# Sparse attention with queries scaled ahead of the split, compressed scores as one 32-column product, and a third pair of FFN blocks by seven products

## The chip, the cores and the metric

The kernel runs on one core of one Trainium2 chip. The metric is the device time of one execution in microseconds. The core's engines are called by their short names in the profile: PE (TensorE: matmuls and transposes into PSUM), PEld (PE's weight loads), DVE (VectorE), ACT (ScalarE), POOL (GpSimd) and SP (SyncE, which issues most DMAs here). Each engine works through its own queue in order and waits for the others by semaphores.

## The reference, cut to what matters

256 tokens, width 1024, two layers. Layer 0 is FFN, stick-breaking attention, FFN; then one shared set of keys and values is computed, with a compression of overlapping blocks of 32 tokens into 15 "compressed" tokens; layer 1 is FFN, sparse attention (16 heads in 4 groups), FFN. All in float32.

```python
h = h + 0.5 * _swiglu(_rmsnorm(h, ffn1_norm[layer]), ffn1_w_in[layer], ffn1_w_out[layer])
...
kvs = _nsa_shared_kv(h, kv_norm, nsa_w_kv, nsa_k_norm, ...)
...
q = _apply_rope(_rmsnorm(q, q_norm), cos, sin)                      # per head, 64 wide
s_c = einsum(q, k_c) * scale                                        # 15 compressed tokens
p_c = softmax(where(valid_c, s_c, NEG)) * any(valid_c)
o_c = einsum(p_c, v_c)
o_s = _nsa_selected(q, sel_idx, k_s, v_s)                           # all 4 blocks of 64 are selected here
o_w = _nsa_window(q, k_w, v_w)
o = gates[0] * o_c + gates[1] * o_s + gates[2] * o_w
```

## The kernel before, in words

**Precision.** Every float32 operand x is split into two float32r parts, hi = round(x) (a copy on ACT) and lo = x - hi (a subtraction on DVE). A product is then three matmuls: hi·hi, hi·lo, lo·hi (`mm3`, L290 to L292). PE does nearly nothing else, and DVE and ACT spend most of their time on splitting weights.

**Weights.** The class `Weights` holds one list of all weight units (128 x 1024, 512 KB) in the order in which they are used. SP loads a unit into a raw buffer, ACT writes its hi (`wh`, L222) and DVE its lo (`wl`, L226), six units ahead at most. `take` hands out the next unit, `done` frees it, `pump` starts the split of a further one. For pairs by seven, some units are sums of weights, which DVE forms beside the splits (L221, L228, L234). A list of jobs, one a unit, also issues DMAs that prepare such sums for the last FFN in DRAM (`far_sums`: moves on SP, L335, and accumulating DMAs on POOL, L338).

**FFN.** The hidden width of 2816 is 11 blocks of 256. A plain block (`proj_block`) is four pieces of twelve matmuls with 512 columns, two for each half of the tokens, and uses four weight units. A "pair by seven" (`pair`) computes two blocks with seven products of twelve matmuls instead of eight, in the manner of Strassen: it uses sums of quarters of the activations (`sums_of_h`) and of the weights, 14 units. A "chunk" is one unit of the second matrix of the FFN (12 matmuls, 22 chunks in all), and chunks are put between the products so that PE has work while DVE prepares weights. The table `FAST` writes this out by hand: a number is a plain block; a tuple is a pair, whose digits are its products, `c` a chunk, `m` a transpose of the gated result (`gtrans`), and `s` a step of the list `side`.

**The changed FFN (f11)**, the first of layer 1: seven plain blocks, then pairs (7, 8) and (9, 10). Beside its plain blocks run the 15 steps of `side` from `kv_phase`: norm and rope of the keys (`k_norm`, `k_scale`, `k_rope`), and the compression: transposes (`c_trans`), the addition of positions on POOL (`c_blocks`, L1224), the split (`c_split`, L1229 and L1230), the hidden product on PE in four steps of two weight units (`c_hidden`, L1246), and what follows it. Step 0 comes after the second piece of the first block; two steps are done per block, after its second and its fourth piece.

**Sparse attention.** The queries are projected in three blocks of heads (`Q_BLOCKS`: head pairs 0-1, 2-4, 5-7). `q_evac` takes them out of PSUM and squares them; `q_turn` applies rope (POOL, L1375 to L1379), splits them (L1380, L1381) and computes the inverse norm `rq` (L1385 to L1392). hi and lo of a head lie side by side, so that one transposed tile `qs` (`q_trans`, L1402 and L1404) holds both along the contraction, and the keys `kD` hold their hi (and their lo) twice along it: two matmuls, against `kh` and `kl`, make a full product. `scores(n)` does the score matmuls of head n for both halves of the tokens (L1417): a mask product, 272 columns (256 keys, 16 compressed) for the first half, 512 keys and 16 compressed columns for the second. Then come the maxima (L1434, L1435), their product with `rq` (L1437), four Exps (L1440, L1445) with the maxima as bias and `rq` as scale, a copy of the compressed scores (L1442), and the normalisation on POOL (L1453). `cmp_soft` is the softmax of the compressed scores of four heads, `ptrans` transposes the probabilities (L1492 to L1495), `values` multiplies by the values. The loop over n puts scores four heads ahead of values; from head 12 on chunks of the output projection come between.

**Order.** A scheduler orders each engine's instructions by their place in the program and by the time at which it expects their inputs; `keep_in_program_order` pins an instruction behind the one traced before it on its engine.

## Time and profile before

| | us |
|---|---|
| three runs | 995.5, 997.32, 995.35; median 995.5 |
| the profiled execution, device time | 994.79 |
| its span, first to last instruction | 993.0 |
| PE busy in the span | 983.4 |
| DVE busy | 873.7 |
| ACT busy | 698.2 |
| POOL busy | 114.9 |

The granted clock of PE is 1.00 throughout. How to read the rows that follow: a group is line, engine, operation, output<-inputs, shape and count, then busy us and the mean ns of one, then the engine's idle time just before and what ended most of it. A row in the order of time is start and length in us, then the same, with the idle time ahead in square brackets. A row of stages is the stretch, its length, and for each engine its busy us with the count of instructions. Durations of neighbouring instructions on one engine overlap, so what one costs is the distance from its start to the next one's.

### The profile page before, as it was taken

To read this page: it belongs to the slowest core of one execution; us is meant where nothing else is said; L and a number is where in the kernel's file an instruction comes from. 1 tells how busy PE (TensorE), PEld (TensorE's weight loads), DVE (VectorE), ACT (ScalarE), POOL (GpSimd) and SP (SyncE) were. 2 spreads that over 40 slices of the span, in tenths; PEclk is the share of its full clock that TensorE was granted. 3 is DMA by queue.
4 is the path that set the end of the run, shared out by engine and by line. 5 is a ranking of instruction groups with operands and counts; after the bars stand their busy time and mean duration, and the time that the engine had idled before them with its cause. 6 is when DMAs were issued, how large, how long until landed. Compare 5 with 4: busy or idle time off the path is not lost.

```text
span 993.0 us, 14093 instructions
## 1 busy us (share of the span) xinstructions
PE 983.4 (99%) x4961; PEld 817.1 (82%) x4961; DVE 873.7 (88%) x1149; ACT 698.2 (70%) x1099; POOL 114.9 (12%) x184
## 2 busy tenths in 40 slices
PE   9999999999999999999999999999999999999998
PEld 6787888898988788878888887888897888788887
DVE  7899999878879999999778698898668879999996
ACT  6776767577868767777565775666669958767763
POOL 0000000010000000000217101000056500000000
PEclk9999999999999999999999999999999999999999
DMA  9988774599846978775996789667330186977761
GB/s 332 355 244 254 222 211 144 176 303 292 247 151 225 332 230 250 235 208 171 273 318 206 252 278 245 235 207 219 114 121 1 45 311 228 310 231 216 250 170 43
DMA packets 65479, 219.89 MB, mean 221 GB/s; under 512 B 7168, under 2 KB 9216, under 8 KB 65408
## 3 DMA queue, kind: packets, MB, share of 16 engines
q1 hardware_dynamic: 58336, 197.86, 58.3%
q0 software_dynamic: 6784, 20.97, 12.1%
q8 instruction: 39, 0.64, 0.3%
q14 instruction: 32, 0.26, 0.1%
q10 hardware_dynamic: 288, 0.16, 0.1%
HBM read 212.67 MB, written 13.63 MB: 228 GB/s over the span
## 4 chain that ended last, share of the span: by engine, by line
PE 69%; issue 13%; DVE 8%; DMA 4%; ACT 3%; POOL 2%; SPq 0%; ACTq 0%; DVEq 0%; POOLq 0%
PE o L291 6%; PE o L292 6%; PE o L290 6%; PE c L290 5%; PE c L292 5%; PE c L291 5%; DVE wl L226 4%; PE a L290 3%; PE a L292 2%; PE a L291 2%; PE cu L290 2%; PE cu L292 2%; PE cu L291 2%; DMA keep<-in_f1i 2%; PE qk L948 2%
## 5 line engine op out<-in xcount | busy, mean ns | idle before, releaser
L226 DVE TENSOR_TENSOR wl<-wraw,wh 128x1024 fp32r<-128x1024 f32 (+2 forms) x316 | 377.1, 1210 | 37.4 <-ACT wh L222 35.7
L222 ACT ACTIVATE wh<-wraw 128x1024 fp32r<-128x1024 f32 (+2 forms) x316 | 322.6, 1044 | 71.1 <-PE o L292 23.8
L222 ACT ACTIVATE wh<-keep 128x1024 fp32r<-128x1024 f32 x112 | 116.6, 1056 | 68.5 <-DVE keep L234 48.8
L226 DVE TENSOR_TENSOR wl<-keep,wh 128x1024 fp32r<-128x1024 f32 x112 | 132.7, 1216 | 6.2 <-ACT wh L222 5.9
L234 DVE TENSOR_TENSOR keep<-keep,wraw 128x1024 f32<-128x1024 f32 x80 | 97.2, 1215 | 1.6 <-DMA wraw<-in_f1i 1.6
L291 PE MATMUL o<-wl,gTh0f 128*128 128x512 f32 x192 | 75.0, 391 | 0.3 <-DVE wl L226 0.3
L290 PE MATMUL o<-wh,gTh0f 128*128 128x512 f32 x192 | 74.8, 397 | 0.0
L292 PE MATMUL o<-wh,gTl0f 128*128 128x512 f32 x192 | 74.6, 391 | 0.0
L290 PE MATMUL o<-wh,gTh1f 128*128 128x512 f32 (+1 forms) x160 | 62.5, 399 | 0.0
L291 PE MATMUL o<-wl,gTh1f 128*128 128x512 f32 (+1 forms) x160 | 62.1, 388 | 0.0
L292 PE MATMUL o<-wh,gTl1f 128*128 128x512 f32 (+1 forms) x160 | 61.3, 388 | 0.0
L290 PE MATMUL a<-wh,hT_f 128*128 128x512 f32 x144 | 57.5, 399 | 0.0
L290 PE MATMUL c<-wh,hT_f 128*128 128x512 f32 x144 | 56.6, 393 | 0.0
L292 PE MATMUL a<-wh,hT_f 128*128 128x512 f32 x144 | 56.3, 391 | 0.0
L291 PE MATMUL a<-wl,hT_f 128*128 128x512 f32 x144 | 56.3, 391 | 0.0
L291 PE MATMUL c<-wl,hT_f 128*128 128x512 f32 x144 | 56.2, 390 | 0.0
L292 PE MATMUL c<-wh,hT_f 128*128 128x512 f32 x144 | 56.2, 390 | 0.0
L290 PE MATMUL cu<-wh,sums 128*128 128x512 f32 x112 | 44.6, 398 | 1.0 <-ACT cp L754 1.0
L290 PE MATMUL c<-wh,sums 128*128 128x512 f32 x112 | 44.3, 396 | 0.1
L292 PE MATMUL cu<-wh,sums 128*128 128x512 f32 x112 | 43.8, 391 | 0.0
L292 PE MATMUL c<-wh,sums 128*128 128x512 f32 x112 | 43.7, 390 | 0.0
L291 PE MATMUL c<-wl,sums 128*128 128x512 f32 x112 | 43.6, 389 | 0.0
(346 smaller groups left out, 2365.0 us busy)
## 6 DMA issues: line engine op xcount, KB each, us to landing
wraw<-in_f1i SPq DMA_DIRECT2D x76, 512.0 KB, 4.8
wraw<-in_f2i SPq DMA_DIRECT2D x68, 512.0 KB, 5.0
wraw<-in_f1o SPq DMA_DIRECT2D x44, 512.0 KB, 4.7
wraw<-in_f2o SPq DMA_DIRECT2D x44, 512.0 KB, 4.8
wraw<-in_sbqk SPq DMA_DIRECT2D x16, 512.0 KB, 4.6
wraw<-sf SPq DMA_DIRECT2D x16, 512.0 KB, 4.5
keep<-in_f2i SPq DMA_DIRECT2D x16, 512.0 KB, 4.5
keep<-in_f2i POOLq DMA_DIRECT2D x16, 512.0 KB, 8.8
```

The source lines that it names most:

```text
L222: i = nc.scalar.activation(hi[:, 0:n], raw[:, 0:n], AF.Copy)
L226: e.tensor_tensor(lo[:, 0:n], raw[:, 0:n], hi[:, 0:n].bitcast(F32), op=OP.subtract)
L234: nc.vector.tensor_tensor(t, y, raw, op=OP.add)
L290: nc.tensor.matmul(o, xh, wh, start=start, stop=False, skip_group_check=True)
L291: nc.tensor.matmul(o, xh, wl, start=False, stop=False, skip_group_check=True)
L292: nc.tensor.matmul(o, xl, wh, start=False, stop=stop, skip_group_check=True)
L948: nc.tensor.matmul(oi, wh[:, c], xh, start=k == 0 and q == 0, stop=False, skip_group_check=True)
```

## The change

Three things are changed together.

1. Blocks 5 and 6 of f11 become a pair by seven; there are five plain blocks and three pairs. The chunks among the pairs are 5, 5 and 6 instead of 7 and 8. The 15 side steps are done three to a plain block (`SIDES`), after its second, third and fourth piece, and the compression's eight weight units move in the list of units (`CMP_AT`).
2. The queries are multiplied by their inverse norm ahead of the split. `q_turn` becomes four steps (rope, norm, scale, split); for query blocks 0 and 1 they are done at once, with rope and scale on DVE, for block 2 one by one in the loop over heads, with rope and scale on POOL. The norm's last steps move from POOL to DVE. The scale drops out of the Exps, and the products of the maxima and of the compressed scores with `rq` are gone.
3. The compressed keys' lo is stored a second time next to the second copy of the hi, so that the second half's two products with 16 columns are one with 32 columns. Its two halves are added later, for four heads at a time (`cmp_max`, split off from `cmp_soft`). `cmp_trans` moves behind `values`.

The letters `p` and `P`, by which a pattern could give a unit's split to POOL, are used in no pattern.

```diff
-CMP_J = 4
+CMP_AT = (12, 12, 14, 16)
+SIDES = (1, 2, 3)
...
-        "f11": (0,1,2,3,4,5,6,(7,"cs1ccm5cc3c67c24"),(9,"cm1cmc5cc3cc67c24")),
+        "f11": (0,1,2,3,4,(5,"1ccm5c3c67c24"),(7,"mc1cm5c3c67c24"),(9,"mc1cmc5c3c67c24")),
...
-    units.extend(f1i1[:4 * CMP_J])
-    cw = len(units)
-    for i in range(4):
-        units.extend(a["cmp"][j] for j in range(2 * i, 2 * i + 2))
-        units.extend(f1i1[4 * CMP_J + 2 * i:4 * CMP_J + 2 * i + 2])
-    units.extend(f1i1[4 * CMP_J + 8:])
+    for i, n in enumerate(CMP_AT + (len(f1i1),)):
+        units.extend(f1i1[CMP_AT[i - 1] if i else 0:n])
+        if i < 4:
+            units.extend(a["cmp"][j] for j in range(2 * i, 2 * i + 2))
...
-                        if i % 2 == 1 and side:
+                        if i in SIDES and side:
...
+            nc.vector.tensor_tensor(kD[0][:, :, 528:544], pv, hi.bitcast(F32), op=OP.subtract)
...
+                e = nc.vector if h0 < 10 else nc.gpsimd
+                return [lambda: q_rope(qv, n, e), lambda: q_norm(sq, n, h0), lambda: q_scale(qv, n, h0, e), lambda: q_split(hi, qv)]
...
+            def q_scale(qv, n, h0, e):
+                e.tensor_tensor(qv, qv, rq[:, :, h0:h0 + n].unsqueeze(3).to_broadcast([P, 2, n, DH]), op=OP.mult)
...
-                nc.gpsimd.tensor_tensor(z, y, y, op=OP.mult)
-                nc.gpsimd.tensor_tensor(z, z, v, op=OP.mult)
-                nc.gpsimd.tensor_scalar(z, z, -0.5, 1.5, op0=OP.mult, op1=OP.add)
-                nc.gpsimd.tensor_tensor(r, y, z, op=OP.mult)
+                nc.vector.tensor_tensor(z, y, y, op=OP.mult)
+                nc.vector.scalar_tensor_tensor(z, z, -0.5, v, op0=OP.mult, op1=OP.mult)
+                nc.vector.scalar_tensor_tensor(r, z, 1.5, y, op0=OP.add, op1=OP.mult)
...
-                mm(sa[:, 272:288], q1, kh[:, 256:272])
                 mm(sv, q1, both(kh), True)
-                mm(sa[:, 272:288], q1, kl[:, 256:272])
                 mm(sv, q1, both(kl))
+                mm(sa[:, 272:304].rearrange("p (t c) -> p t c", t=2), q1,
+                   kh.rearrange("p (t c) -> p t c", t=2)[:, :, 256:272])
...
-                m = nm[:, 0, :].rearrange("p (t b) -> p t b", t=2)
-                nc.vector.tensor_tensor(m, m, r.unsqueeze(2).to_broadcast([P, 2, 2]), op=OP.mult)
...
-                                         scale=r[:, 0:1], accum_out=nm[:, 1, b:b + 1])
+                                         accum_out=nm[:, 1, b:b + 1])
...
+            def cmp_max(sc):
+                nc.vector.tensor_tensor(cs[sc][:, 1], cs[sc][:, 1], cs[sc][:, 2], op=OP.add)
...
-                nc.gpsimd.tensor_tensor(cs[sc], cs[sc], rq[:, :, 4 * sc:4 * sc + 4].unsqueeze(3).to_broadcast([P, 2, 4, 16]),
-                                        op=OP.mult)
...
                 if n == 1:
-                    turn()
-                if n == 3:
+                    rope()
+                if n == 4:
                     q_trans(2, (5,))
...
                 if n + 4 < 16:
                     scores(n + 4)
+                if n == 1:
+                    norm()
+                if n == 2:
+                    scale()
+                if n == 3:
+                    split()
...
                 values(n - 1)
+                if n % 4 == 3:
+                    cmp_trans(sc)
```

More of the change, by code (lines that the diff above doesn't have):

```diff
@@ L82, in __init__ @@
         self.key, self.load, self.join, self.last = key, load, join, last
-        self.more = ()
+        self.more, self.slow = (), False
 class Unit:
@@ L90, in __init__ @@
         self.ap, self.key, self.of, self.hold, self.held = ap, key, of, hold, held
-        self.more = ()
+        self.more, self.slow = (), False
 class Weights:
@@ L224, in pump @@
             self.tc.keep_in_program_order(i)
-        e = nc.gpsimd if u in self.on_pool else nc.vector
+        e = nc.gpsimd if not isinstance(x, bass.AP) and x.slow else nc.vector
         e.tensor_tensor(lo[:, 0:n], raw[:, 0:n], hi[:, 0:n].bitcast(F32), op=OP.subtract)
@@ L403, in fast @@
                     v += b(n.pop(0), 1)
+                elif ch in "pP":
+                    for d in range(-1 - (ch == "P"), 0):
+                        if isinstance(v[d], bass.AP):
+                            v[d] = Unit(v[d])
+                        v[d].slow = True
                 elif ch in "tx":
@@ L480, in build @@
     msb = cp.tile([P, P], BF, name="msb")
-    mns = cp.tile([P, 320], BF, name="mns")[:, 0:288]
+    mns = cp.tile([P, 320], BF, name="mns")[:, 0:304]
     def consts():
@@ L492, in consts @@
         nc.vector.tensor_copy(mns[:, 256:288], msk[:, M_C:M_C + 32])
+        nc.gpsimd.memset(mns[:, 288:304], 0.0)
     ssq = {}
@@ L1344, in nsa @@
                 nc.gpsimd.memset(x[64:128].bitcast(F32), 0.0)
-            qw, Pm, PT, cs, Ox = {}, {}, {}, {}, {}
+            qw, Pm, PT, cs, cm, Ox = {}, {}, {}, {}, {}, {}
             heads = [(2 * sc + i, hh) for sc in range(4) for hh in range(2) for i in range(2)]
@@ L1409, in scores @@
                 if n % 4 == 0:
-                    cs[sc] = sp.tile([P, 2, 4, 16], F32, tag="cs", bufs=2, name="cs")
+                    cs[sc] = sp.tile([P, 3, 4, 16], F32, tag="cs", bufs=2, name="cs")
                 g = 2 * (p // 4) + hh
@@ L1420, in scores @@
                 sv = sb.rearrange("p (t c) -> p t c", t=2)
-                mm(sa[:, 0:288], identb, mns, True)
+                mm(sa[:, 0:304], identb, mns, True)
                 mm(sa[:, 0:272], q0, kh[:, 0:272])
                 mm(sa[:, 0:272], q0, kl[:, 0:272])
-                mm(sa[:, 272:288], q1, kh[:, 256:272])
                 mm(sv, q1, both(kh), True)
-                mm(sa[:, 272:288], q1, kl[:, 256:272])
                 mm(sv, q1, both(kl))
+                mm(sa[:, 272:304].rearrange("p (t c) -> p t c", t=2), q1,
+                   kh.rearrange("p (t c) -> p t c", t=2)[:, :, 256:272])
                 mm(sb[:, 256:512], identb, mns[:, 0:256])
@@ L1446, in scores @@
                                          vb[:, b, :, :], AF.Exp, bias=nm[:, 0, 2 + b:3 + b],
-                                         scale=r[:, 1:2], accum_out=nm[:, 1, 2 + b:3 + b])
+                                         accum_out=nm[:, 1, 2 + b:3 + b])
                 f = nm[:, 2, :].rearrange("p (t b) -> p t b", t=2)
@@ L1453, in scores, with cmp_soft @@
                     nc.gpsimd.tensor_tensor(x, x, nm[:, 2, j:j + 2].unsqueeze(2).to_broadcast([P, 2, w]), op=OP.mult)
-            def cmp_soft(sc):
-                v = cs[sc].rearrange("p t n i -> p (t n) i")
-                mx = sp.tile([P, 2, 8], F32, tag="cm", bufs=2, name="cm")
+            def cmp_max(sc):
+                nc.vector.tensor_tensor(cs[sc][:, 1], cs[sc][:, 1], cs[sc][:, 2], op=OP.add)
+                v = cs[sc][:, 0:2].rearrange("p t n i -> p (t n) i")
+                mx = cm[sc] = sp.tile([P, 2, 8], F32, tag="cm", bufs=2, name="cm")
                 nc.vector.tensor_reduce(mx[:, 0, :], v, axis=AX.X, op=OP.max)
                 nc.gpsimd.tensor_tensor(v, v, mx[:, 0, :].unsqueeze(2).to_broadcast([P, 8, 16]), op=OP.subtract)
-                nc.gpsimd.tensor_tensor(cs[sc], cs[sc], rq[:, :, 4 * sc:4 * sc + 4].unsqueeze(3).to_broadcast([P, 2, 4, 16]),
-                                        op=OP.mult)
+            def cmp_soft(sc):
+                v = cs[sc][:, 0:2].rearrange("p t n i -> p (t n) i")
+                mx = cm[sc]
                 nc.scalar.activation(v, v, AF.Exp)
@@ L1536, in nsa @@
                 turn = q_evac(b, o)
-                if b < 2 or not True:
-                    turn()
+                while b < 2 and turn:
+                    turn.pop(0)()
+            rope, norm, scale, split = turn
             oo = None
@@ L1571, in nsa @@
                 if n == 1 or n % 4 == 0:
+                    cmp_max(sc)
                     cmp_soft(sc)
-                if n % 4 == 3:
-                    cmp_trans(sc)
                 if n + 1 < 16:
```

17 lines of the change are left out of this document (8 added, 9 removed).

## The prediction, made before the changed kernel was run

> **What bounds the kernel now.** I read the page first, for the engines' shares, then busy time by stage, then groups of instructions by shape, last the order of time around the places that the change touches.
>
> ```profile
> PE 983.4 (99%) x4961; PEld 817.1 (82%) x4961; DVE 873.7 (88%) x1149; ACT 698.2 (70%) x1099; POOL 114.9 (12%) x184
> ```
>
> TensorE (PE) is busy for 983.4 of 993.0 us. Since matmuls are pipelined, that alone does not say that a removed matmul shortens the run; the stages do. The next rows are busy time by stage: the second FFN of layer 0 (310 to 440), the plain blocks of the FFN that changes (515.9 to 610), its two pairs (610 to 690), the query projection (710 to 745.5) and the sparse attention's heads (745.5 to 789).
>
> ```profile
> core 0: us, PE busy (x) PEld busy (x) DVE busy (x) ACT busy (x) POOL busy (x), PEclk, DMA share, GB/s
> 310.00:440.00 130.00, 129.18 (x583) 105.30 (x582) 128.00 (x141) 97.41 (x124) 7.59 (x9) 1.00 0.82 258
> ...
> 515.90:568.00 52.10, 52.10 (x252) 43.50 (x251) 41.35 (x53) 33.14 (x45) 23.77 (x28) 1.00 0.76 226
> 568.00:610.00 42.00, 41.93 (x225) 34.50 (x224) 34.05 (x46) 27.45 (x37) 2.27 (x6) 1.00 0.88 283
> 610.00:690.00 80.00, 80.00 (x358) 65.61 (x358) 73.38 (x75) 53.92 (x65) 0.90 (x1) 1.00 0.69 217
> ...
> 710.00:745.50 35.50, 35.26 (x231) 32.48 (x230) 26.95 (x57) 26.49 (x65) 15.45 (x32) 1.00 0.41 130
> 745.50:789.00 43.50, 41.33 (x275) 34.57 (x274) 34.84 (x92) 42.28 (x158) 27.92 (x56) 1.00 0.03 9
> ```
>
> From 515.9 to 690 PE idles 0.07 us: there the run gets shorter by what PE is spared, if VectorE (DVE) keeps up. From 745.5 to 789 ScalarE (ACT) is busy for 42.28 of 43.50 us and PE idles 2.17: ACT sets that stage, and PE's savings alone are worth little in it.
>
> **The third pair by seven.** Two plain blocks are 96 matmuls of 512 columns; a pair is seven products of twelve, 84. Neighbours in the order of time start 0.23 us apart:
>
> ```profile
> 604.08 0.39 PE L291 MATMUL a<-wl,hT_f 128*128 128x512 f32 x1
> 604.31 0.39 PE L292 MATMUL a<-wh,hT_f 128*128 128x512 f32 x1
> ```
>
> 12 x 0.23 = 2.8 us less on PE. The price is on DVE (rows of the two pairs, 610 to 690):
>
> ```profile
> L226 DVE TENSOR_TENSOR wl<-wraw,wh 128x1024 fp32r<-128x1024 f32 x29 | 34.6, 1217 | 1.9 <-ACT wh L222 1.7
> ...
> L234 DVE TENSOR_TENSOR keep<-keep,wraw 128x1024 f32<-128x1024 f32 x8 | 9.7, 1215 | 1.6 <-DMA wraw<-in_f1i 1.6
> L221 DVE TENSOR_TENSOR wraw<-wraw,wraw 128x1024 f32<-128x1024 f32 x4 | 4.9, 1219 | 0.1
> ...
> L656 DVE SCALAR_TENSOR_TENSOR g<-x,sil 128x256 f32<-128x256 f32 x4 | 1.7, 418 | 0.0
> L759 DVE TENSOR_TENSOR x<-cu,cp 128x512 f32<-128x512 f32 x2 | 1.4, 684 | 0.0
> ```
>
> A pair takes 14 weight units where two blocks take 8: six more splits at 1.22, eight sums of weights (L234 and L221's kind) at 1.22 and two sums of results at 0.68, together 18.5 us of DVE, and six splits and four copies on ACT, which is busy for 53.9 of 80 there. Cover: DVE idles 10.8 + 8.0 + 6.6 = 25.4 us between 515.9 and 690, so it would be busy for about 96% of it. The 310 row shows this kernel with DVE at 128.0 of 130 us and PE idle for 0.82. Lower bound 0. Upper bound: the pairs by themselves, with nothing ready ahead. The third pair and the one chunk more that is put among the pairs bring 15 splits and 8 sums at 1.22, four passes at 0.68 and four gates at 0.42, 32.5 us, against PE's eight products of twelve and two transposes, 23; 73.4 + 32.5 is 3 us over PE's 80 + 23. I take 0.8, the 310 row's, as the nearest. DMA: two transfers of 512 KB more on SP's queue, since the pair reads one quarter of its weights twice; the share of the DMA engines is 0.69 there, so 0.
>
> **One 32-column product.** Per head, two 16-column products become one of 32 columns:
>
> ```profile
> 727.63 0.51 PE L1417 MATMUL S<-kDh,qs 128*128 128x16 f32 x2
> 727.97 0.51 PE L1417 MATMUL S<-kDl,qs 128*128 128x16 f32 x2
> 728.32 0.28 PE L1417 MATMUL S<-mns,identb 128*128 128x256 bf16 x1
> ...
> L1417 PE MATMUL S<-mns,identb 128*128 128x288 bf16 x16 | 4.7, 294 | 0.3 <-ACT cs L1442 0.3
> L1417 PE MATMUL S<-mns,identb 128*128 128x256 bf16 x16 | 4.5, 281 | 0.0
> ```
>
> A pair of 16 and 512 columns takes 0.34 us from start to start, 0.11 more than 512 alone; 16 x 0.11 = 1.8 us of PE. The mask's 16 more columns cost at most 13 ns a head (288 against 256), 0.1 in all, set against it. The evacuated scores grow by 16 columns and get one small addition per four heads.
>
> **Norm ahead of the split.** With the queries scaled beforehand, the 64 Exps lose their per-partition scale, 16 small DVE products go, and four POOL products:
>
> ```profile
> L1440 ACT ACTIVATE P<-S,nm,rq 128x128 f32<-128x128 f32 x32 | 15.0, 486 | 0.8 <-DVE nm L1437 0.8
> L1445 ACT ACTIVATE P<-S,nm,rq 128x256 f32<-128x256 f32 x32 | 18.4, 602 | 0.0
> L1463 ACT ACTIVATE cs<-cs 128x128 f32<-128x128 f32 x4 | 1.3, 325 | 0.7 <-POOL cs L1461 0.7
> L1359 ACT ACTIVATE qsq<-qp,rstd 128x384 f32<-128x384 f32 x4 | 2.4, 591 | 2.7 <-DVE qw L1356 2.7
> L1494 ACT ACTIVATE PT<-pt 128x384 fp32r<-128x384 f32 x16 | 8.0, 506 | 0.9 <-PE pt L1492 0.9
> ...
> L1437 DVE TENSOR_TENSOR nm<-nm,rq 128x4 f32<-128x4 f32 x16 | 3.3, 207 | 0.2
> L1461 POOL TENSOR_TENSOR cs<-cs,rq 128x128 f32<-128x128 f32 x4 | 1.6, 405 | 0.3
> ```
>
> No row shows this Exp with one operand less. An Exp of the same shape with neither bias nor scale takes 325 ns (L1463) against 486 (L1440): 161 for two, 80 for one. A Square with a scale takes 591, a Copy of that shape without one 506: 85. Lower bound 0 (the functions and the sources differ), upper 85. I take 80: 64 x 0.08 = 5.1 us of ACT, of which 48 Exps of twelve heads, 3.8 us, lie between 745.5 and 789. The Trainium skill (ScalarE: Activation LUTs, What ACT_TABLE_LOAD costs) gives about 93 ns for each such operand; by that the 64 are worth 6.0 us, the stage below would reach PE's bound of 3.5, and the sum would be -5.4.
>
> What is late next there is PE: it needs 41.33 - 12 x 0.11 = 40.0 us, so the stage can shrink by 3.5 at most. DVE (34.8) and POOL (27.9) have room. I take 3.0, since PE and ACT alternate in dependence. The heads ahead of 745.5 give 4 x 0.11 = 0.4, on a PE that idles 0.24 us. Together -3.4; bounds -0.4 and, with the other 16 Exps' 1.3 us and the whole 3.5, -5.2.
>
> Against it stands a longer way of the first queries. Rope moves from POOL to DVE for query blocks 0 and 1, and the norm comes ahead of the split:
>
> ```profile
> 719.38 1.06 POOL L1375 TENSOR_TENSOR qr<-qw,cst 128x128 f32<-128x128 f32 x1 [5.08 <-DVE qw L1356]
> ...
> 721.06 0.46 POOL L1379 TENSOR_TENSOR qw<-qr 128x128 f32<-128x128 f32 x1
> ...
> 720.43 0.67 DVE L1385 TENSOR_REDUCE qn<-qsq 128x8 f32<-128x512 f32 x1
> ...
> 722.22 0.69 DVE L1381 TENSOR_TENSOR qw<-qw 128x512 f32<-128x512 f32 x1 [0.46 <-ACT qw L1380]
> ...
> 724.28 1.03 PE L1402 MATMUL qTp<-cst,qw 128*128 128x128 f32 x8
> ...
> 727.07 0.34 PE L292 MATMUL qp<-wh,hT_m 128*128 128x384 f32 x1
> ```
>
> Rope's four steps take 2.1 us on POOL; on DVE four at 0.2 (L1437's) are 0.8. Added are a reduction of 0.67, six small steps of 0.2 on DVE and ACT, and a scaling like L1381's 0.69: 2.6. The transposes that follow (724.28) come 1.3 us later; the projection's last piece, up to 727.07, can go ahead of them, so it costs 0, and 1.3 if PE's order keeps the transposes first. Block 2's rope stays on POOL, its scaling goes there too (six times L1461's size: 2.4 us), and its steps spread over the first three heads; the scores that need it are those of head 8, four heads later: 0.
>
> **The compression beside five blocks.** Fifteen side steps now lie beside five plain blocks, three a block, and the first product of the compression (L1246) comes after 11 pieces of plain block instead of 16:
>
> ```profile
> 525.31 3.90 POOL L1224 TENSOR_TENSOR kvb<-kvb,vec 128x120 f32<-128x120 f32 x4
> ...
> 539.62 0.98 POOL L338 DMA_DIRECT2D sf<-in_f2i  x1
> 547.65 0.91 POOL L338 DMA_DIRECT2D sf<-in_f2i  x1 [7.05 <-DMA wraw<-in_cmp]
> 549.12 1.68 POOL L1224 TENSOR_TENSOR kvb<-kvb,vec 128x120 f32<-128x120 f32 x4 [0.56 <-DVE hT_xb L1230]
> ...
> 558.61 1.05 ACT L1229 ACTIVATE hT_xb<-kvb 128x1024 fp32r<-128x1024 f32 x1
> ...
> 559.87 1.22 DVE L1230 TENSOR_TENSOR hT_xb<-kvb,hT_xb 128x1024 fp32r<-128x1024 f32 x1
> ...
> 562.74 0.28 PE L1246 MATMUL hid<-wh,hT_xb 128*128 128x256 f32 x1
> ```
>
> Five pieces of 12 x 0.23 and a transpose step of 0.4 are 14.2 us, so the product falls due at 548.5 instead of 562.7. It needs the eight additions for the second half (L1224) and their split (L1229, L1230: 2.3 us). The additions of 549.12 were released by DVE's split of the first half, not by the DMA issue that ends 0.56 us ahead of them. That split moves up by three pieces, 8.3 us, to about 540.7; additions (2 x 1.68) and split then end at 546.4, in time. Bounds: 0, and the 10 us that the slower rival works out. I take 0.5, near the lower end, by that row.
>
> **Sum.** -2.8 + 0.8 - 3.4 + 0.5 = -4.9. The profiled execution took 994.8, so 989.9; the runs' median of 995.5 is 0.7 above it, so 990.6, put at 990.5.
>
> **Rivals.** *POOL's queue delays the compression (slower).* The accumulating DMA of 547.65 sits 7.05 us in POOL's queue behind the one of 539.62. If the additions stand behind it, as now, they begin at 548.6 however early their input is, and end with their split 5.7 us later if they go as at 549.12, or 10.1 later if as at 525.31 (3.90 for four): 5.8 to 10.2 us after they are due. With no other work for PE the middle, 8, makes -5.4 + 8.0 = +2.6: 998.1. It decides for slower from a stall of 7.4 us on. The Trainium skill (GPSIMD Engine Reference, Key points) says that GpSimd shares its SBUF interfaces with VectorE and contends with its two-input instructions; 3.90 against 1.68 us for the same four would fit it, and by that rule the longer end holds, 10.2, and 1000.3. Against the rival: 549.12 names DVE, not the queue, and PE may take the next piece first. *DVE becomes the bound of the three pairs.* It is at 73.4 of 80 already; at its upper 3 us the pair earns nothing: 992.8. The 310 row speaks against it. *The heads do not shrink.* If the Exps' time does not fall, or PE's waits there are of order and not of ACT, only 0.4 remains of 3.4: 993.6.
>
> **Chances.** The forecast 0.57 (988 to 992.5); the heads 0.15 (half faster, half within 0.2%); DVE 0.13 (0.08 faster, 0.05 within); POOL's queue 0.15 (0.09 slower, 0.06 within). The 0.2%, 2 us, is about what a measurement of this kernel tells from no change. Faster 0.72, same 0.19, slower 0.09. The range goes from 987.5 (all gains at their ends and no new stall, -8.0) to 997 (the lower part of the queue rival).
>
> **What would show it.** Exps near 406 and 522 ns; ACT no longer over 95% busy through the heads, PE above it; the heads' stage near 40.5 us; 12 matmuls of 512 columns and 16 of 16 columns fewer; DVE about 96% busy in the changed FFN with PE idle under 1 us; no idle of PE ahead of L1246's product. A PE wait there, or on weight splits in the first of the three pairs, or Exps of the same length, would make me wrong.

## The result, and the profile after

The changed kernel takes 1003.19 us (median; 1002.68 to 1003.47), the kernel before 995.51 beside it: ratio 1.007, 95% interval 1.0056 to 1.0085. The forecast was 990.5, so the change is slower where I had given that 0.09. Measured once more on another chip it was 1003.52, ratio 1.0075 (1.0057 to 1.0092).

I cut both profiled executions at three products of TensorE: the first of the changed FFN, the first of the query projection, the first of the last FFN. These rows are from the order of time, first of before, then of after (start, duration, engine, line, operation).

```profile
515.87 0.39 PE L290 MATMUL a<-wh,hT_f 128*128 128x512 f32 x1
...
710.26 0.39 PE L290 MATMUL qp<-wh,hT_m 128*128 128x304 f32 x1
...
816.43 0.48 PE L290 MATMUL a<-wh,hT_f 128*128 128x512 f32 x1
```

```profile
516.89 0.39 PE L290 MATMUL a<-wh,hT_f 128*128 128x512 f32 x1
...
718.43 0.39 PE L290 MATMUL qp<-wh,hT_m 128*128 128x304 f32 x1
...
824.67 0.48 PE L290 MATMUL a<-wh,hT_f 128*128 128x512 f32 x1
```

| stage, us | before | after | difference | forecast |
|---|---|---|---|---|
| up to the changed FFN | 515.9 | 516.9 | +1.0 | 0 |
| changed FFN, compression beside it | 194.4 | 201.5 | +7.1 | -1.5 |
| sparse attention | 106.2 | 106.2 | 0.1 | -3.4 |
| last FFN to the end | 176.6 | 177.0 | +0.4 | 0 |

The first row is no effect of the change: nothing is different up to there, and over the profiled executions of this study the changed FFN (or its counterpart) starts between 514.3 and 517.5, but for the one kernel that changes an earlier FFN. The second execution of the changed kernel has 516.0 there, and again 201.5 for the FFN.

The page's line of shares after:

```profile
PE 980.2 (98%) x4933; PEld 811.8 (81%) x4933; DVE 893.3 (89%) x1173; ACT 700.2 (70%) x1109; POOL 110.9 (11%) x162
```

The 28 matmuls are gone (4961 to 4933), as forecast. The time went into waits. These are TensorE's waits in the changed FFN after (who waits, for whom: us in all, times, longest; the longer ones), first beside the plain blocks, then in the three pairs:

```profile
PE xtp L1212 <- DVE kva L1209: 1.8, 1, 1.8
PE gTp L669 <- DVE kDl L1196: 0.9, 1, 0.9
PE gTp L669 <- DVE g L661: 0.7, 1, 0.7
```

```profile
PE c L291 <- DVE wl L226: 1.5, 1, 1.5
PE cu L290 <- ACT cp L757: 1.5, 1, 1.5
```

Before, the stage had PE idle for 0.07 us up to 690. Two different places, then: transposes of the compression and of the plain blocks that wait for VectorE, and products of the pairs that wait for weights or for a copy.

### The profile page after: what moved, and what is told of

Same layout as the page of the kernel before. It is cut to its first block, busy times and chain, and to the rows that moved or that the text cites. A ratio compares the mean times of both kernels' runs of the same rounds, so it can differ in the third digit from the quotient of the medians.

```text
span 1001.7 us, 14034 instructions
## 1 busy us (share of the span) xinstructions
PE 980.2 (98%) x4933; PEld 811.8 (81%) x4933; DVE 893.3 (89%) x1173; ACT 700.2 (70%) x1109; POOL 110.9 (11%) x162
## 4 chain that ended last, share of the span: by engine, by line
PE 63%; issue 15%; DVE 11%; DMA 5%; ACT 2%; POOL 2%; SPq 0%; DVEq 0%; POOLq 0%; ACTq 0%
PE o L291 6%; PE o L292 6%; PE o L290 6%; PE c L290 5%; PE c L292 5%; PE c L291 5%; DVE wl L226 5%; PE cu L290 2%; PE cu L292 2%; PE cu L291 2%; DMA wraw<-in_f1i 2%; PE qk L951 2%; PE qk L952 1%; PE qk L953 1%; PE gTp L669 1%
## 5 line engine op out<-in xcount | busy, mean ns | idle before, releaser
L222 ACT ACTIVATE wh<-keep 128x1024 fp32r<-128x1024 f32 x120 | 125.5, 1056 | 70.5 <-DVE keep L234 49.5
L226 DVE TENSOR_TENSOR wl<-keep,wh 128x1024 fp32r<-128x1024 f32 x120 | 142.4, 1217 | 7.2 <-ACT wh L222 6.8
L234 DVE TENSOR_TENSOR keep<-keep,wraw 128x1024 f32<-128x1024 f32 x84 | 102.1, 1216 | 1.9 <-DMA wraw<-in_f1i 1.9
L292 PE MATMUL o<-wh,gTl0f 128*128 128x512 f32 x192 | 74.5, 391 | 0.0
L291 PE MATMUL c<-wl,hT_f 128*128 128x512 f32 x156 | 61.1, 392 | 1.5 <-DVE wl L226 1.5
L290 PE MATMUL c<-wh,hT_f 128*128 128x512 f32 x156 | 61.3, 393 | 0.0
L292 PE MATMUL c<-wh,hT_f 128*128 128x512 f32 x156 | 60.8, 390 | 0.0
L290 PE MATMUL a<-wh,hT_f 128*128 128x512 f32 x112 | 45.1, 402 | 0.0
L291 PE MATMUL a<-wl,hT_f 128*128 128x512 f32 x112 | 43.9, 392 | 0.0
L292 PE MATMUL a<-wh,hT_f 128*128 128x512 f32 x112 | 43.8, 391 | 0.0
```

Of the source, the lines that this page charges most:

```text
L222: i = nc.scalar.activation(hi[:, 0:n], raw[:, 0:n], AF.Copy)
L226: e.tensor_tensor(lo[:, 0:n], raw[:, 0:n], hi[:, 0:n].bitcast(F32), op=OP.subtract)
L234: nc.vector.tensor_tensor(t, y, raw, op=OP.add)
L290: nc.tensor.matmul(o, xh, wh, start=start, stop=False, skip_group_check=True)
L291: nc.tensor.matmul(o, xh, wl, start=False, stop=False, skip_group_check=True)
L292: nc.tensor.matmul(o, xl, wh, start=False, stop=stop, skip_group_check=True)
```

## The experiments

Theory: the FFN part of the change carries the loss, half of it by the denser side steps, half by the third pair; the sparse attention gains what was forecast and gives it back in its last heads. All times are medians; the ratio is to the kernel before on the same chip.

| run | us | ratio, 95% | changed FFN | sparse attention |
|---|---|---|---|---|
| ffn_only | 1000.75 | 1.0035 to 1.0065 | 200.8 | 106.1 |
| sides_only | 998.98 | 1.0022 to 1.0049 | 198.3 | 106.1 |
| ffn_late | 999.43 | 1.0024 to 1.0050 | 197.1 | 105.8 |
| nsa_only | 994.97 | 0.9986 to 1.0006 | 194.4 | 107.5 |
| norm_only | 993.57 | 0.9973 to 0.9992 | 194.3 | 104.2 |
| nsa_cmp | 992.27 | 0.9951 to 0.9976 | 194.5 | 103.7 |
| nsa_cmp_n | 994.27 | 0.9979 to 1.0000 | 194.4 | 106.0 |
| nsa_add | 993.60 | 0.9970 to 0.9991 | 194.4 | 105.7 |
| combo | 995.20 | 0.9989 to 1.0006 | 198.1 | 103.7 |
| after_again | 1003.52 | 1.0057 to 1.0092 | 201.5 | 107.5 |
| ffn_skip7 | 1000.91 | 1.0039 to 1.0064 | 200.3 | 106.1 |
| skip_mid | 999.77 | 1.0028 to 1.0055 | 195.5 | 106.1 |
| skip_all | 997.56 | 1.0013 to 1.0032 | 195.4 | 106.2 |
| pair_mid | 1003.25 | 1.0064 to 1.0088 | 199.3 | 106.1 |
| pair_cp2 | 1002.18 | 1.0054 to 1.0082 | 200.1 | 105.9 |
| combo_mid | 995.61 | 0.9991 to 1.0013 | 199.8 | 103.8 |
| ffn_pool | 1018.89 | 1.0216 to 1.0256 | 218.4 | 106.0 |
| f20_narrow | 1001.12 | 1.0041 to 1.0066 | 194.3 | 106.1 |

The stage columns are the profiled execution's, cut as above.

### Which part carries the loss

**The FFN part alone (ffn_only).** Before, with this edit:

```
-CMP_J = 4
+CMP_AT = (12, 12, 14, 16)
+SIDES = (1, 2, 3)
...
-        "f11": (0,1,2,3,4,5,6,(7,"cs1ccm5cc3c67c24"),(9,"cm1cmc5cc3cc67c24")),
+        "f11": (0,1,2,3,4,(5,"1ccm5c3c67c24"),(7,"mc1cm5c3c67c24"),(9,"mc1cmc5c3c67c24")),
...
-                        if i % 2 == 1 and side:
+                        if i in SIDES and side:
```

> The kernel before with only the FFN part of the change (third pair by seven, three side steps of the compression beside each of five plain blocks). Theory A, the FFN part carries the loss: its stage was 7.2 us longer in the changed kernel (201.5 against 194.4 from its first product to the first of the query projection), so about 1002.7, +7. Rival B, the sparse attention's part carries it, by way of what it does to weights and buffers around it: then about 993 to 995.

**The sparse attention's part alone (nsa_only).** After, with the lines above put back.

> The changed kernel with its FFN part undone: norm ahead of the split and the 32-column product alone. Theory A: the stage took 106.2 us before and after, so 995.5 within 1.0, although the Exps are shorter by 90 ns each. Rival B: 999 or more. My prediction's own step would give 992.1 (-3.4).

**The side steps alone (sides_only).** As ffn_only, with before's f11 line: five blocks with three side steps each, two without, two pairs.

> The kernel before with two pairs as it had them, and only the compression packed three side steps beside each of the first five plain blocks (two plain blocks and the pairs then follow without side steps). Theory A1, the packing makes VectorE late for the transposes: stalls of PE as in the changed kernel between 530 and 590 us, about 5 in all, so 1000 to 1001. Theory A2, the third pair alone makes the loss (VectorE or the weights' path is the bound of three pairs): 995 to 996.5 here.

Measured: +5.5, -0.3, +3.7; the first and the last are 1 to 2 us below what was expected. The FFN part carries the loss, and the side steps alone make most of it. TensorE's longer waits in that kernel's seven plain blocks are those of the changed kernel; before has none there:

```profile
PE xtp L1208 <- DVE kva L1205: 1.9, 1, 1.9
PE gTp L665 <- DVE kDl L1192: 0.7, 1, 0.7
```

Its blocks, up to the first product of the first pair, take 99.2 us against 94.8: 4.4 more. The third pair then adds 1.8 on top (1000.75 against 998.98), where -2.8 + 0.8, so 2.0 less, was forecast.

**The whole again (after_again).**

> The changed kernel once more, on the chip of the next three. The two parts alone stood at +5.5 (FFN part, 1000.75) and -0.3 (sparse attention's part, 994.97), the whole at +7.7. Theory, the parts add up: 1000 to 1001.5. Rival, they work on each other (an addition of 2 us or more): 1002.5 to 1003.5.

1003.52: the sum of the parts' medians, +5.2, falls short of +7.8. By the stages it does not: +6.4 for the FFN of ffn_only and +1.3 for the sparse attention of nsa_only make 7.7. The sparse attention of the changed kernel took 106.2 in one execution and 107.5 in the other. The traces show what differs: the granted clock. In after_again's, ahead of 796.52, TensorE has waited 2.0 us as in the first execution, but then its clock stands at 0.50 for 3.41 us, and products of 512 columns start 0.43 us apart instead of 0.23 (a row of stages; the clock is the third number from its end):

```profile
797.50:800.80 3.30, 3.30 (x11) 2.73 (x10) 3.25 (x5) 3.30 (x6) 0.00 (x0) 0.50 0.42 149
```

That execution has a second such stretch at 650.63; nsa_only's has one, at 788.84; before's, ffn_only's and the first of the changed kernel have none. In the profiled executions a mean clock of 0.998 or less goes with such a stretch, and a higher one with none. By that sign all six executions of after_again have one, four of nsa_only's twelve (median 996.6, the others 994.4), one of ffn_only's six and none of before's 23 beside pair_mid. So a wait of TensorE can cost more than its own length, through the clock. How much of the missing 2.6 us this makes was not separated: the first execution of the changed kernel has none and took 1003.46.

### The side steps

This is VectorE in the order of time after, around TensorE's longest wait, then TensorE; below it the same copies before:

```profile
526.37 1.49 DVE L1173 TENSOR_TENSOR kva<-kva,ksr 128x1024 f32<-128x1024 f32 x1 [2.40 <-POOL ksr L1168]
...
531.64 1.00 DVE L1209 COPY kva<-kva 128x256 f32<-128x256 f32 x2
...
542.38 0.94 DVE L1209 COPY kva<-kva 128x256 f32<-128x256 f32 x2
...
543.47 0.30 PE L1212 MATMUL xtp<-cst,kva 128*128 128x128 f32 x1 [1.82 <-DVE kva L1209]
```

```profile
532.62 0.72 DVE L1206 COPY kva<-kva 128x256 f32<-128x256 f32 x2
...
545.61 0.49 DVE L1206 COPY kva<-kva 128x256 f32<-128x256 f32 x2
```

After, the copy that the transposes need (542.38) stands at the end of a row without a gap over 0.1 us that begins at 526.37 with the scaling of the keys. Before, the same copy for the same transposes came 13 us after the one ahead of it; now 10.7, with all else in between.

**The side steps spread two, two, three, four, four (ffn_late).** With ffn_only's edit, and:

```
-CMP_AT = (12, 12, 14, 16)
-SIDES = (1, 2, 3)
+CMP_AT = (13, 14, 15, 16)
+SIDES = ((1, 3), (1, 3), (1, 2, 3), (0, 1, 2, 3), (0, 1, 2, 3))
-                        if i in SIDES and side:
+                        if j < len(SIDES) and i in SIDES[j] and side:
```

By this CMP_AT two of the compression's weights and two of a block's change places, so its values are others; instructions and bytes are as many. 

> The kernel before with the FFN part, but the fifteen side steps spread two, two, three, four, four over the five blocks (the normalization, scaling and duplication of the compressed keys, heavy on VectorE, as far apart as before; the compression's products closer together later). Base: the FFN part alone, 1000.75. Theory A1, VectorE's pile between 526 and 545 us makes the stalls of 0.8 and 2.0 us of the transposes: 997.5 to 998.5. Rival, the work is merely put off and the same 3 to 4 us of waits return two blocks later: within 1 of 1000.75.

The waits at 532 and 540 are gone, and the blocks take 70.8 us against 74.5, 3.6 less; a wait of 1.35 us for a split inside the compression's product takes their place, at 555.9. The median fell by 1.3 only, less than the theory had it and more than the rival; the two intervals overlap. The stage shows it: by the median alone this repair is not told from no change.

### The sparse attention

The Exps, in groups by line, after (busy us, mean ns):

```profile
L1456 ACT ACTIVATE P<-S,nm 128x256 f32<-128x256 f32 x32 | 15.6, 518 | 0.0
L1451 ACT ACTIVATE P<-S,nm 128x128 f32<-128x128 f32 x32 | 11.9, 391 | 0.9 <-DVE nm L1447 0.8
```

602 to 518 and 486 to 391: 84 and 95 ns less each. From the first score product to the last it is 53.4 us against 55.1, and up to the first 16.1 against 17.0. Then comes this (GpSimd, ScalarE, TensorE and VectorE after, each in the order of time):

```profile
793.28 2.61 POOL L1464 TENSOR_TENSOR P<-P,nm 128x256 f32<-128x256 f32 x2
795.85 0.40 POOL L1472 TENSOR_TENSOR cs<-cs,cm 128x128 f32<-128x128 f32 x1
...
796.28 0.31 ACT L1478 ACTIVATE cs<-cs 128x128 f32<-128x128 f32 x1 [2.75 <-POOL cs L1472]
...
797.52 0.52 PE L1507 MATMUL pt<-cst,P 128*128 128x128 f32 x3 [2.02 <-DVE cm L1480]
...
791.67 0.45 DVE L1468 TENSOR_TENSOR cs<-cs 128x64 f32<-128x64 f32 x1
792.09 0.18 DVE L1460 RECIPROCAL nm<-nm 128x4 f32<-128x4 f32 x1
792.19 0.26 DVE L1471 TENSOR_REDUCE cm<-cs 128x8 f32<-128x128 f32 x1
```

Before, VectorE and GpSimd at the same place:

```profile
787.06 0.27 DVE L1459 TENSOR_REDUCE cm<-cs 128x8 f32<-128x128 f32 x1
787.36 0.18 DVE L1449 RECIPROCAL nm<-nm 128x4 f32<-128x4 f32 x1
...
787.41 0.41 POOL L1460 TENSOR_TENSOR cs<-cs,cm 128x128 f32<-128x128 f32 x1 [1.82 <-DVE cm L1459]
```

After, the maximum of the last four heads' compressed scores (L1471) is there at 792.45, but its subtraction (L1472) stands on GpSimd behind head 15's scaling (L1464), since head 15's reciprocal (L1460) now comes ahead of the maximum: the new addition (L1468) is what put the maximum off. Before, the maximum came first, and the subtraction at 787.41 went ahead of that scaling, at 788.54. ScalarE's queue then stands for 2.75 us at the Exp of these scores, with the rounding behind it that TensorE's next transposes need.

**The subtraction on VectorE (nsa_cmp).** nsa_only, and for the last four heads:

```
-                nc.gpsimd.tensor_tensor(v, v, mx[:, 0, :].unsqueeze(2).to_broadcast([P, 8, 16]), op=OP.subtract)
+                (nc.vector if sc == 3 else nc.gpsimd).tensor_tensor(v, v, mx[:, 0, :].unsqueeze(2).to_broadcast([P, 8, 16]), op=OP.subtract)
```

> As the kernel with the sparse attention's part alone, but the subtraction of the maximum of the last four heads' compressed scores goes on VectorE instead of GpSimd, where it stands behind 2.6 us of scaling of head 15. Theory C, that order is what gives back the heads' gain (PE stall of 2.2 us at 795 in the changed kernel, ScalarE idle 2.7): 2 us less than that kernel. Rival D, the gain is lost in the last heads whatever the order, since transposes and values wait for the scaling of heads 14 and 15 on GpSimd: within 0.5 of it.

**The norm without the 32-column product (norm_only).** nsa_only with before's two 16-column products, so without the addition:

```
-                nc.vector.tensor_tensor(cs[sc][:, 1], cs[sc][:, 1], cs[sc][:, 2], op=OP.add)
```

> The norm ahead of the split alone: two 16-column products a head as before, no addition of their two parts. Theory C, the added addition on VectorE puts the maximum's subtraction for the last four heads behind head 15's scaling on GpSimd; without it the subtraction stands ahead again, the 2.2 us of PE wait at 795 us go, and only the products' 0.11 us a head stay: 993 to 994, below both parts together (994.97). Rival, the shorter Exps bring the wait whatever the order: 995 to 996.

Both as the theory has it: 992.27 and 993.57. In norm_only the subtraction stands ahead of head 15's scaling on GpSimd, as before the change. TensorE's waits over the sparse attention of nsa_cmp; the one of 2.0 us is gone and no other came:

```profile
PE pt L1507 <- DVE hT_m L1510: 1.2, 2, 0.8
PE qTp L1416 <- DVE qw L1394: 0.5, 1, 0.5
```

nsa_cmp is faster than both kernels of this case (ratio to before 0.9964, 0.9951 to 0.9976). These rows of stages are the whole sparse attention of before, norm_only and nsa_cmp:

```profile
710.26:816.43 106.17, 103.76 (x644) 89.58 (x642) 82.60 (x176) 85.53 (x248) 46.63 (x92) 1.00 0.36 119
...
711.18:815.35 104.17, 103.22 (x644) 89.53 (x642) 84.75 (x180) 79.83 (x246) 43.37 (x69) 1.00 0.37 126
...
709.38:813.09 103.71, 101.36 (x628) 87.51 (x626) 85.70 (x184) 80.30 (x246) 41.51 (x68) 1.00 0.37 126
```

They tell the two parts apart. The norm ahead of the split (norm_only) takes TensorE's idle time from 2.4 us to 0.95. The 32-column product then spares TensorE 1.9 us of work, and brings back 1.4 us of idle time.

**Two tries at the 1.2 us that are left.** In nsa_cmp_n the last query block's norm goes back to GpSimd; in nsa_add the addition goes there for the first twelve heads.

```
+                if h0 < 10:
...
+                else:
+                    nc.gpsimd.tensor_tensor(z, y, y, op=OP.mult)
+                    nc.gpsimd.tensor_tensor(z, z, v, op=OP.mult)
+                    nc.gpsimd.tensor_scalar(z, z, -0.5, 1.5, op0=OP.mult, op1=OP.add)
+                    nc.gpsimd.tensor_tensor(r, y, z, op=OP.mult)
```

```
-                nc.vector.tensor_tensor(cs[sc][:, 1], cs[sc][:, 1], cs[sc][:, 2], op=OP.add)
+                (nc.vector if sc == 3 else nc.gpsimd).tensor_tensor(cs[sc][:, 1], cs[sc][:, 1], cs[sc][:, 2], op=OP.add)
```

> As the kernel with the subtraction on VectorE (992.27), and the four small steps of the norm of the last query block on GpSimd as before instead of three on VectorE, where they took 0.4 to 0.7 us each for 24 or 12 columns beside GpSimd's scaling. Theory, they are what makes VectorE late for the value products at 755 and 759 us (1.5 us of PE wait): 991 to 991.7. Rival, ScalarE bounds those heads (33.9 of 35.9 us) and PE's waits only move: within 0.5 of 992.27.

> As the kernel with the subtraction on VectorE (992.27), and the addition of the two parts of the compressed scores on GpSimd for the first three groups of heads, where it took 1.10 us on VectorE beside GpSimd's scaling. Theory, that addition makes VectorE late for the value products at 746 and 750 us (1.2 us of PE wait, absent in the kernel without the addition): 991 to 991.5. Rival, GpSimd's queue takes it over, as with the norm's steps: 992 to 994.5.

994.27 and 993.60. nsa_add's rival holds; nsa_cmp_n is 2.0 us above its base, which neither of its theories gave. GpSimd's queue passes the steps on late: the transposes of the last queries wait 1.2 us for their split in nsa_cmp_n and 1.9 in nsa_add (0.5 in nsa_cmp). In both profiled executions a stretch of 3.41 us at clock 0.50 follows (at 760.19 and 759.79). By the mean clock eight of nsa_cmp_n's twelve executions and six of nsa_add's twelve have one, none of nsa_cmp's five; the medians of the others are 993.6 and 992.8.

### The third pair

The theory at first was that VectorE has too much to do in the pairs. Seven kernels show how far that goes; P1 to P7 in the expectations are names of this section's theories.

**Seven weight splits on GpSimd (ffn_pool).** ffn_only, with a "p" behind seven of the chunks, whose splits then go to GpSimd:

```
-(5,"1ccm5c3c67c24"),(7,"mc1cm5c3c67c24"),(9,"mc1cmc5c3c67c24")
+(5,"1cpcm5cp3c67cp24"),(7,"mcp1cm5cp3c67cp24"),(9,"mcp1cmc5c3c67c24")
```

> The kernel before with the FFN part, and seven of the sixteen chunks' weight splits among the three pairs on GpSimd, idle there, instead of VectorE (8.5 us of VectorE's work). Theory P1, VectorE is the bound in the second and third pair: their stalls, 4.9 us in all, fall by 3 or more, 996.5 to 998. Rival P2, the wait is the chain sum, rounding, subtraction, product, with too few units ahead, and a GpSimd split of some 3 us only makes it longer: 1000 to 1004.

1018.89, outside both. A split takes 4.06 us on GpSimd (1.22 on VectorE), VectorE's own work gets longer beside it, and TensorE idles 13.1 us in the pairs, 6.4 of them in one place for such a split; its clock is at 0.50 for 10.2 us of that stretch, partly during these waits (groups of lines, then waits):

```profile
L226 POOL TENSOR_TENSOR wl<-wraw,wh 128x1024 fp32r<-128x1024 f32 x7 | 28.4, 4064 | 81.2 <-ACT wh L222 74.2 <-DVE x L761 7.0
...
L234 DVE TENSOR_TENSOR keep<-keep,wraw 128x1024 f32<-128x1024 f32 x9 | 14.5, 1615 | 0.7 <-DMA wraw<-in_f1i 0.7
...
PE o L291 <- POOL wl L226: 6.4, 1, 6.4
```

**Seven, then twelve subtractions left out (ffn_skip7, skip_mid).** The products of the units marked with "p" (the last two units by "P") use the rounded part twice, so the values are others and the products as many. ffn_skip7 has the seven marks of ffn_pool, skip_mid "5cp3Pcp67" in each pair:

```
+        if not isinstance(x, bass.AP) and x.slow:
+            self.lo[u] = hi
+        else:
+            nc.vector.tensor_tensor(lo[:, 0:n], raw[:, 0:n], hi[:, 0:n].bitcast(F32), op=OP.subtract)
...
```

> The kernel before with the FFN part; seven chunks among the three pairs use their rounded weights in place of the low part too, whose subtraction is left out (8.5 us less of VectorE's work; the products are as many). Base 1000.75. Theory P1, VectorE's work is what the second and third pair wait for (4.9 us of stalls at 646 to 666 us, and 0.5 at 612): 996 to 997.5, with these stalls under 1.5 in all. Rival P2, the chain of a sum, its rounding and its subtraction is too long for the units that are ready ahead, however busy VectorE is: 999.5 to 1001.

> The kernel before with the FFN part; in each pair the two chunks between the second and the sixth product and the two units of the third product use their rounded part in place of the low part, whose subtraction is left out (4.9 us less of VectorE's work in that stretch of each pair). Theories P1 and P3: the stalls there fall under 1.5 of 4.9, 996.5 to 998. Theory P5, the copy behind ScalarE's five roundings is what counts: 1000 to 1001, as with the seven chunks left out elsewhere.

The first is 1000.91, no gain: the waits moved from between 646 and 666 us to, mostly, between 684 and 687. The second shows not one wait over 0.25 us in the pairs, 122.3 us from the first pair's first product to the query projection against 126.3 in ffn_only. But that execution, 996.0, is the fastest of twelve that reach to 1002.9, and their median, 999.77, is not apart from ffn_only's. By itself it settles nothing.

**A chunk moved behind the second product (pair_mid).** ffn_only, with:

```
-(5,"1ccm5c3c67c24"),(7,"mc1cm5c3c67c24"),(9,"mc1cmc5c3c67c24")
+(5,"1cm5cc3c67c24"),(7,"mc1m5cc3c67c24"),(9,"mc1cm5cc3c67c24")
```

> The kernel before with the FFN part (1000.75); in each of the three pairs one chunk moves from ahead of the second product to behind it, as before's pairs had it; as many chunks in all. Theory P3, the stretch from the second product to the sixth and seventh is too short for VectorE (10 splits, 2 sums of kept and 2 of loaded weights, gates: 20 us, against 16.6 of PE with two chunks, 19.4 with three): stalls in the pairs fall by 2.5 or more, 997 to 998.5. Theory P1, VectorE's load over all the pairs counts: 1000 to 1001.5.

**ScalarE's copy ahead of two roundings (pair_cp2).** In the changed kernel, the copy that the seventh product waits for stands behind five roundings (ScalarE, then TensorE, in the order of time):

```profile
644.18 3.14 ACT L222 ACTIVATE wh<-wraw 128x1024 fp32r<-128x1024 f32 x3 [3.50 <-DVE wraw L221]
647.70 1.06 ACT L222 ACTIVATE wh<-wraw 128x1024 fp32r<-128x1024 f32 x1 [0.38 <-DMA wraw<-in_f1i]
649.93 1.06 ACT L222 ACTIVATE wh<-wraw 128x1024 fp32r<-128x1024 f32 x1 [1.17 <-DMA wraw<-in_f1i]
650.89 0.58 ACT L757 ACTIVATE cp<-cu 128x512 f32<-128x512 f32 x1
...
651.52 0.50 PE L290 MATMUL cu<-wh,hT_xb 128*128 128x512 f32 x1 [1.49 <-ACT cp L757]
```

```
+                    tc.keep_in_program_order(nc.scalar.activation(y, st["u"], AF.Copy))
+                    W.pin = True
+                    W.pump()
+                    W.pump()
+                    W.pin = False
...
```

(The last two roundings are held back until the copy is queued.) 

> The kernel before with the FFN part; the copy of the sixth product's result, which the seventh waits for, stands on ScalarE ahead of the last two of the five roundings it stood behind. Theory P5, the queue's order makes the waits of 1.5 to 1.7 us for that copy: 1.2 to 3 us less than 1000.75, 997.8 to 999.5. Theories P1 and P3, VectorE is late and the wait only passes to a weight's low part: within 0.8 of 1000.75.

1003.25 and 1002.18, no gain in either, and both above what any of their theories gave; why is open. Each profiled execution is the fastest of its six (999.36 and 1000.22). With the copy moved, the waits pass to roundings and splits (0.5 us at 645, 0.8 at 663): the order of ScalarE's queue is not the cause by itself, it shows where the lateness lands. The place of the chunks does not help either.

**Twenty-eight subtractions cut to 8 columns (skip_all).** All sixteen chunks and the units of "3" and "2" in the pairs; the values are others here too.

```
+        few = not isinstance(x, bass.AP) and x.slow
+        m = 8 if few else n
+        nc.vector.tensor_tensor(lo[:, 0:m], raw[:, 0:m], hi[:, 0:m].bitcast(F32), op=OP.subtract)
+        if few:
+            self.lo[u] = hi
```

> The kernel before with the FFN part; the sixteen chunks of the three pairs and the units of their third and second-to-last products (28 units) use the rounded part in place of the low part, of which only 8 columns are subtracted, so that VectorE still lets go of each buffer in the old order (31 us less of its work among 127). Theory P1/P3, VectorE's work makes the pairs' waits: none over 0.5 us, the pairs 122.3 us as with the twelve left out, and 995.5 to 997.5 in the median, not in the profiled run alone. Theory P7, transfers and the few buffers make them, in an execution more, in another less: 999 or more, with a spread of 4 us or more.

997.56, at the upper end of what the first theory gave (995.5 to 997.5) and 3.2 less than ffn_only, and TensorE does not idle in the pairs. Busy time by stretch from the first pair to the query projection, ffn_only and then skip_all (stretch, length, then busy us and instructions of PE, PEld, DVE, ACT, POOL; clock, DMA share, GB/s):

```profile
589.20:640.00 50.80, 50.62 (x228) 41.52 (x228) 46.74 (x50) 33.11 (x41) 1.86 (x2) 1.00 0.69 220
640.00:670.00 30.00, 27.27 (x122) 21.60 (x121) 26.78 (x28) 19.77 (x25) 0.00 (x0) 1.00 0.68 233
670.00:715.60 45.60, 45.60 (x211) 37.24 (x210) 40.32 (x49) 27.81 (x41) 0.59 (x2) 1.00 0.56 186
```

```profile
588.40:640.00 51.60, 51.60 (x233) 42.50 (x233) 37.15 (x52) 36.72 (x47) 1.86 (x2) 1.00 0.73 240
640.00:670.00 30.00, 30.00 (x137) 24.68 (x136) 23.64 (x33) 20.89 (x26) 0.00 (x0) 1.00 0.67 244
670.00:710.80 40.80, 40.80 (x191) 33.33 (x189) 28.20 (x42) 24.54 (x37) 0.59 (x2) 1.00 0.50 164
```

VectorE's work falls from 113.8 us to 89.0 and the stretch from 126.4 to 122.4. So without these subtractions of VectorE the pairs do not wait. But 113.8 of 126.4 is 90%, less than the 128.0 of 130 that the second FFN of layer 0 bears with 0.8 us of idle. What has that FFN that this one lacks?

**The second FFN of layer 0 with as few buffers (f20_narrow).** It has 8 buffers of loaded and 8 of split weights; the changed FFN, with the compression's data in SBUF, has 5 and 6. Before, with:

```
-        spans.append((n, len(units)))
+        if l != "f20":
+            spans.append((n, len(units)))
```

> The kernel before, with the second FFN of layer 0 (five pairs, no compression beside it) given the buffers that the changed FFN has: 5 of loaded and 6 of split weights, instead of 8 and 8. Theory P7, few units ahead make the pairs' waits: that FFN, which waits 0.8 us between 310 and 440 with its eight, gets 4 to 12 us longer, 999.5 to 1007.5. Rival, the number ahead does not matter (VectorE's sum of work does, 128.0 of 130 us in either): within 1.5 of 995.5.

1001.12, +5.6. The waits in that FFN, between 310 and 446 us, and its stretch of 310 to 440:

```profile
PE o L290 <- ACT wh L222: 2.1, 1, 2.1
PE cu L290 <- ACT cp L755: 1.4, 2, 1.0
...
310.00:440.00 130.00, 125.48 (x554) 101.15 (x553) 122.76 (x134) 92.83 (x117) 5.92 (x8) 0.99 0.75 236
```

They are of the kinds seen in the changed FFN's pairs: for the copy, for roundings, for splits. A stretch at clock 0.50 follows the first of them (336.63 to 340.04) in this execution; the four others have a mean clock of 1.00 and take 999.8 to 1001.4. The same work for VectorE, 98% of its time with eight units ahead, holds TensorE up with six. So the likely account has two halves: pairs fill VectorE almost as full as TensorE, and with few units ahead each uneven stretch of that reaches TensorE. Each half is shown in one of the two FFNs; that more units ahead would free the changed FFN was not run. That transfers and buffers make the waits whatever VectorE has to do (P7 as skip_all was to show it, 999 or more) fell; that the number of units ahead counts (P7 as f20_narrow was to show it) stood. Which of the two rings it is, and how much of skip_all's gain is the load and how much the shorter chain of its 28 units, was not separated.

### Both repairs together

combo is the changed kernel with nsa_cmp's line and ffn_late's steps (CMP_AT (14, 14, 16, 16), so that all weights are in place); combo_mid has pair_mid's f11 line besides.

> The whole change with two repairs: side steps two, two, three, four, four to a block, and the last maximum's subtraction on VectorE. By the stages of the single runs (FFN 3.6 us shorter than in the FFN part alone, sparse attention 3.8 shorter than in its part alone), 995 to 997 against the changed kernel's 1003.2. Rival, the repairs only move waits when both parts are there: above 999.

> The whole change with the two repairs (995.2) and the chunks moved as in the kernel with the FFN part. Theory P3: 992 to 993.5. Theory P1: 994.5 to 996.

995.20: the two repairs take back 8.3 us, the whole loss (7.4 by the stages of the profiled executions); 995.61: the moved chunks add nothing. What stays against nsa_cmp's 992.27 is the FFN: 198.1 us against 194.5.

## Why the prediction was wrong

**The third pair (-2.8 + 0.8).** The 2.8 us of TensorE are there: twelve matmuls of 512 columns fewer, at 0.23. VectorE's added work is near the 18.5 us worked out (176.95 us busy in the changed FFN, 160.13 before). Its price, 0.8 with 3 as upper bound, was mis-sized: the pairs of ffn_only take 126.3 us against 122.3 without a wait, 4.0. The step that failed is "I take 0.8, the 310 row's, as the nearest". It is the nearest in busy share, but its FFN has 8 and 8 buffers where this one has 5 and 6, and with those it is itself 6.3 us longer. The upper bound, from sums of busy time, could not show a wait that comes from order and few units ahead. The rival "DVE becomes the bound of the three pairs" is the nearer one, and it was priced too low.

**The compression beside five blocks (+0.5, bounds 0 and 10).** Measured 4.4 by stage, 3.7 by the medians: inside the bounds, at the wrong end, and by another mechanism. I followed what the compression's first product needs, and that was in time (TensorE does not wait at it); GpSimd's queue did not delay it either, since its additions went ahead of the second accumulating DMA:

```profile
545.41 2.30 POOL L1227 TENSOR_TENSOR kvb<-kvb,vec 128x120 f32<-128x120 f32 x4 [0.39 <-ACT kvb L1216]
547.65 0.98 POOL L338 DMA_DIRECT2D sf<-in_f2i  x1
```

What I did not follow is VectorE's queue: three steps a block bring half again as many steps to it, and the transposes of the steps and of the blocks wait there.

**The sparse attention (-3.4).** The Exps lost 84 and 95 ns (forecast 80). The Trainium skill (ScalarE: Activation LUTs, What ACT_TABLE_LOAD costs) gives about 93 ns for each such operand, and the mean of the two rows, 90, is nearer to that than to my 80. The product spared TensorE 1.9 us (forecast 1.8). From the projection's last product to the last Exp it is 42.4 us against 45.6, 3.2 less where I took 3.0. With the last wait repaired the stage is 2.5 us shorter and the run 3.0 (nsa_cmp). Not all of it came as worked out: between these two TensorE still idles 2.2 us, as before the change. The waits for ScalarE that the shorter Exps were to end did go (norm_only), but waits for VectorE took their place, and 1.2 us of TensorE's work moved behind the last Exp. The step that failed is the one without a price: "get one small addition per four heads". Of itself it is 0.20 us of VectorE alone and 0.45 to 1.10 beside GpSimd's scaling; what it cost is 2.0 us of TensorE in the last heads, since it changed which of two small results reaches GpSimd's queue first, and in nsa_cmp another 1.2 for which VectorE comes late to the probabilities (with the addition on GpSimd, in nsa_add, 0.2 of these is left). The queries' longer way (0) cost nothing: the first score product comes 0.9 us earlier. Block 2's moved steps (0) left a wait of 0.5.

**The sum.** With the sizes of the runs, -2.8 + 4.0 + 4.4 for the FFN and nothing for the sparse attention make +5.6; ffn_only has +5.5 by the medians and +6.4 by its stage. The changed kernel's FFN is 0.7 longer than ffn_only's in both executions, which is not explained, and stretches at clock 0.50 come on top in some.

## What to carry to other kernels

A row that shows VectorE at 98% without waits holds for its own depth of buffers: before taking a price from another stage, compare how many units each has ready ahead. When steps are packed closer, add up what each engine's queue gets per block, not only when the next consumer's input is ready. A small operation added ahead of a shared in-order queue is priced by what slips ahead of it there, not by its own duration. A wait of TensorE can cost more than its length: look at the granted clock behind it.

## What the runs showed of the hardware

Small additions and multiplications of VectorE from SBUF (12 and 64 columns) last until the GpSimd scaling beside them is over. The same TENSOR_SCALAR of 12 columns takes 0.17 us alone and 0.74 during a scaling that ends at 758.46, 0.03 ahead of it; the addition of 64 columns at 754.31 takes 1.10 us and ends 0.1 us after GpSimd's. VectorE's reciprocals and reductions are not held: L1460's of 792.09 takes 0.18 us during a scaling that lasts to 793.04 (GpSimd, then VectorE, changed kernel):

```profile
756.85 1.61 POOL L1464 TENSOR_TENSOR P<-P,nm 128x256 f32<-128x256 f32 x2
...
737.97 0.17 DVE L1401 TENSOR_SCALAR qn<-qn 128x12 f32<-128x12 f32 x1
...
757.75 0.74 DVE L1401 TENSOR_SCALAR qn<-qn 128x12 f32<-128x12 f32 x1
```

The Trainium skill (GPSIMD Engine Reference, Key points) says that GpSimd shares its SBUF interfaces with VectorE; the 1615 ns of VectorE's sums beside GpSimd's splits in ffn_pool, 1218 in ffn_only, agree.

In seven profiled executions of this study the granted clock of TensorE falls to 0.50 for 3.41 us (in ffn_pool once for 6.83), each time in a wait of TensorE or at most 1.3 us behind one of 0.8 us or more. Not each such wait brings it: behind the 2.02 us ahead of 797.52 in the changed kernel's first execution the clock stays at 1.00. The kernel before, without a wait over 1 us between 20 and 970 us, has no such stretch.

One profiled execution can stand far from its kernel's median: skip_mid's twelve cover 6.9 us, before's 23 beside them 4.2, and its profiled one is 3.8 us below the median.
